# Row maximum of a 64 MiB tensor: the loads cut as 14, 14, 12, 11, 9, 8, 8, ... in two blocks, in place of 15, 14, 13, 11, ... in four

## Chip, cores and metric

One core of a Trainium2 chip. The metric is the device time of one execution in microseconds (us). The span that the profile shows is some 2 us shorter. DVE is the vector engine, which does the reductions.

## The reference

```python
x = np.random.randn(32, 512, 1024).astype(np.float32)   # drawn with a fixed seed
return np.max(x, axis=-1).astype(np.float32)            # 32 x 512 results
```

16384 rows of 1024 floats: 128 partitions with 128 rows each. Below, "a row" is one row in each of the 128 partitions, 512 KiB in all.

## The kernel before

```python
BLOCKS = [
    [15, 14, 13],
    [11, 9, 8, 7],
    [6, 6, 5, 4, 4, 4, 3, 2],
    [2, 2, 2, 2, 2, 1, 1, 1, 1, 1, 1, 1],
]
RING = 46
...
    ring = once.tile([P, RING, D], F32)
    res = once.tile([P, I], F32)
    at = first = 0
    for loads in BLOCKS:
        S = sum(loads)
        xb = xf[first * P:(first + S) * P, :].rearrange("(p i) d -> p i d", p=P)
        b = 0
        for g in loads:
            if at + g > RING:
                at = 0
            xc = ring[:, at:at + g, :]
            nc.sync.dma_start(out=xc, in_=xb[:, b:b + g, :])
            nc.vector.reduce_max(out=res[:, first + b:first + b + g], in_=xc, axis=X)
            at += g
            b += g
        dst = bass.AP(tensor=of.tensor, offset=of.offset + first * P, ap=[[S, P], [1, S]])
        nc.scalar.dma_start(out=dst, in_=res[:, first:first + S])
        first += S
```

A block of S rows gives each partition S consecutive rows, so neighbouring partitions read S x 4 KiB apart: that is the pitch. Each block ends with one output. Within a block each number is one load and one reduction. The sizes fall because a row takes longer to load than to reduce (1.204 against 1.067 us, worked out in the prediction): each reduction should last about as long as the next, smaller load.

Of the kernel before, what the change touches and what calls it, by code (L numbers as in the profile page):

```python
# [1 line left out]

# [4 lines left out]


F32 = mybir.dt.float32



BLOCKS = [
    [15, 14, 13],
    [11, 9, 8, 7],
    [6, 6, 5, 4, 4, 4, 3, 2],
    [2, 2, 2, 2, 2, 1, 1, 1, 1, 1, 1, 1],
]
RING = 46


@with_exitstack
def kernel(
    ctx: ExitStack,
    tc: tile.TileContext,
    x: bass.AP,
    out: bass.AP,
):
    nc = tc.nc
    P = 128  # L30
    X = mybir.AxisListType.X

    xf = x.flatten_outer_dims()
    N, D = xf.shape
    I = N // P
    of = out.flatten_outer_dims()

    once = ctx.enter_context(tc.tile_pool(name="once", bufs=1))
# [19 lines that stand above are left out]
    assert first == I  # L58


# [1 line left out]
_INS = ['x']  # L62
_OUTS = [((32, 512), 'float32')]


# [23 lines left out]
```

## Time and profile before

| | before |
|---|---|
| time, first three runs | 165.55 to 165.71 us, median 165.6 |
| span of the profiled run | 163.6 us |
| DVE busy, of the span | 138.4 us, 85% |
| load queue, share of 16 engines | 96.3% |
| loads, reductions, outputs | 27, 27, 4 |
| first reduction starts; last one ends | 21.39; 161.25 us |

Neither resource has slack: the stream of loads is full from 1.7 to 159.1 us, and the DVE works without a pause from 54.06 to the end.

### The profile page before, as it was taken

What the parts mean: (1) busy time and instruction counts of PE and PEld (TensorE: products, weight loads), DVE (VectorE), ACT (ScalarE), POOL (GpSimd) and SP (SyncE); (2) the same over time, 40 slices, a digit from 0 to 9 for tenths busy, and PEclk for the clock granted to TensorE, in tenths of its full rate; (3) what the DMA queues carried; (4) which work ended last, traced back from release to release, by engine and by line L of the source; (5) the groups of instructions that cost most, each with busy time, mean ns of one, the idle gap of its engine ahead of it and who ended that gap; (6) DMA issues with size and microseconds to landing.
All of it is one profiled execution on the core that took longest, in us unless ns stands there. A gap on an engine that the chain in (4) does not pass through costs nothing.

```text
span 163.6 us, 114 instructions
## 1 busy us (share of the span) xinstructions
DVE 138.4 (85%) x27; POOL 0.2 (0%) x4
## 2 busy tenths in 40 slices
DVE  0000079998999899999999999999999999999994
POOL 0000000000000000000000000000000000000000
DMA  7999699999999989999989999999999999999980
GB/s 240 481 481 436 285 449 449 449 449 417 417 417 417 529 353 529 388 425 401 459 385 465 449 401 427 439 400 459 419 421 421 445 405 421 421 421 415 409 339 2
DMA packets 4464, 67.18 MB, mean 411 GB/s; under 512 B 1008, under 2 KB 1008, under 8 KB 1904
## 3 DMA queue, kind: packets, MB, share of 16 engines
q1 hardware_dynamic: 3888, 67.11, 96.3%
q10 hardware_dynamic: 576, 0.07, 0.3%
HBM read 67.11 MB, written 0.07 MB: 411 GB/s over the span
## 4 chain that ended last, share of the span: by engine, by line
DVE 74%; DMA 23%; DVEq 1%; another core or an unknown queue 0%; SPq 0%; issue 0%
DVE res L52 74%; DMA ring<-in_x_dram 23%; DVEq L84 1%; SPq L51 0%
## 5 line engine op out<-in xcount | busy, mean ns | idle before, releaser
L52 DVE TENSOR_REDUCE res<-ring 128x1 f32<-128x1024 f32 (+12 forms) x27 | 138.4, 5205 | 22.8 <-DMA ring<-in_x_dram 22.8
L73 POOL MEMSET const-bfloat16-1.0<- 128x1 bf16 x1 | 0.1, 102 | 0.0
L73 POOL MEMSET const-uint8-127<- 128x1 uint8 x1 | 0.1, 102 | 0.0
L73 POOL MEMSET const-float32-0.0<- 128x1 f32 x1 | 0.1, 99 | 0.2 <-issue 0.2
L73 POOL MEMSET const-float32-1.0<- 128x1 f32 x1 | 0.1, 99 | 0.0
## 6 DMA issues: line engine op xcount, KB each, us to landing
ring<-in_x_dram SPq DMA_DIRECT2D x1, 7680.0 KB, 20.6
ring<-in_x_dram SPq DMA_DIRECT2D x1, 7168.0 KB, 37.2
ring<-in_x_dram SPq DMA_DIRECT2D x1, 6656.0 KB, 52.4
ring<-in_x_dram SPq DMA_DIRECT2D x2, 3072.0 KB, 33.3
ring<-in_x_dram SPq DMA_DIRECT2D x3, 2048.0 KB, 33.8
ring<-in_x_dram SPq DMA_DIRECT2D x6, 1024.0 KB, 23.9
ring<-in_x_dram SPq DMA_DIRECT2D x1, 5632.0 KB, 29.8
ring<-in_x_dram SPq DMA_DIRECT2D x1, 4608.0 KB, 24.9
```

Of the source, the lines that this page charges most:

```text
L52: nc.vector.reduce_max(out=res[:, first + b:first + b + g], in_=xc, axis=X)
L73: nc = _bacc.Bacc("TRN2", target_bir_lowering=False, num_devices=1)
L84: with _tile.TileContext(nc) as tc:
```

## The change

Its intent is to keep reductions and loads in step with one load fewer and two outputs fewer.

```diff
 BLOCKS = [
-    [15, 14, 13],
-    [11, 9, 8, 7],
-    [6, 6, 5, 4, 4, 4, 3, 2],
-    [2, 2, 2, 2, 2, 1, 1, 1, 1, 1, 1, 1],
+    [14, 14, 12, 11, 9, 8, 8, 7, 6, 5, 4, 4, 4, 3, 3],
+    [2, 2, 2, 2, 2, 1, 1, 1, 1, 1, 1],
 ]
```

Four things move at once: the load sizes, their number (27 to 26), the outputs (4 to 2), and the pitches (168, 140, 136 and 68 KiB become 448 and 64 KiB).

## The prediction

> **What bounds the kernel now.** I read the page first: busy time by engine and the transfer queues, for which resource is full.
>
> ```profile
> span 163.6 us, 114 instructions
> DVE 138.4 (85%) x27; POOL 0.2 (0%) x4
> ...
> q1 hardware_dynamic: 3888, 67.11, 96.3%
> q10 hardware_dynamic: 576, 0.07, 0.3%
> ```
>
> The load queue (q1) is full for 96.3% of the span, the vector engine (DVE) for 85%. So this is a stream of 64 MiB with a reduction running behind it. To see whether the stream ever pauses I asked for the stretch from its first packet (1.7 us) to its last (159.1 us). The columns are stretch, length, DVE busy, POOL busy, clock, transfer share, GB/s.
>
> ```profile
> 1.70:159.10 157.40, 136.28 (x26) 0.00 (x0) 1.00 1.00 427
> ```
>
> It does not pause: share 1.00. The dip near the fifth slice of the page's timeline is only how packets are binned by their start. Next, the chain of waits that ended last, in order of time.
>
> ```profile
> 0.73 0.37 SPq L51
> 1.10 0.05 issue
> 1.15 37.16 DMA ring<-in_x_dram
> 38.31 0.02 issue
> 38.33 15.09 DVE res L52
> 53.42 0.61 another core or an unknown queue
> 54.03 0.02 issue
> 54.06 106.07 DVE res L52 x24
> 160.12 1.13 DVEq L84
> ```
>
> From 54.06 us on the DVE never waits: 25 reductions end at 161.25. So the end is set by the third load's landing (54.03) plus all work after it, although the stream is also full until 159.1. The two bounds nearly touch: by the trace's semaphore record the last one-row load landed at 159.57, and its reduction started at 160.03, when the one before let it, only 0.46 us later. Last, cost per shape (shape, busy and mean ns, idle before it).
>
> ```profile
> L52 DVE TENSOR_REDUCE res<-ring 128x15 f32<-128x15360 f32 x1 | 16.2, 16153 | 21.4 <-DMA ring<-in_x_dram 21.4
> L52 DVE TENSOR_REDUCE res<-ring 128x14 f32<-128x14336 f32 x1 | 15.1, 15087 | 0.8 <-DMA ring<-in_x_dram 0.8
> L52 DVE TENSOR_REDUCE res<-ring 128x13 f32<-128x13312 f32 x1 | 14.0, 14020 | 0.6 <-DMA ring<-in_x_dram 0.6
> ```
>
> A row more costs 16153 - 15087 = 1066 ns. The 0.8 and 0.6 us are the DVE waiting for loads 2 and 3; nothing later has idle time.
>
> **What the Trainium skill says.** "VectorE: DVE Perf Modes", section "The perf-mode tier table (the rule you actually need)": tensor_reduce has only the 1x program. With the 0.96 GHz that the page gives, 1024 elements are 1067 ns; the trace's 1066 agrees, so cutting the loads otherwise cannot make a row cheaper. "DMA: Bandwidth & Descriptors", section "Where 436 GB/s comes from", gives a ceiling of 435 GB/s; the trace moves 427 over the whole stream, so only 2% is left there, part of which is overhead per descriptor. The same page, section "Latency and other measured facts", reports row pitches of large powers of two that slow copies between HBM tensors: 207 GB/s per direction at 512 KiB against 214 for a padded one, 164 at 2 MiB. That bears on the new blocks, whose pitch is 112 x 4 = 448 KiB and 16 x 4 = 64 KiB per partition, against 168, 140, 136 and 68 before. The trace before has nothing on it: its four blocks run at one rate.
>
> **A model from the trace.** Let n be rows landed and k loads landed. Three landings, 38.31 (29 rows, 2 loads), 54.03 (42, 3) and 159.57 (128, 27), give two slopes. From 54.03 - 38.31 = 15.72 = 13a + b and 159.57 - 54.03 = 105.54 = 86a + 24b follow a = 1.204 us per row and b = 0.08 per load; the constant is then 3.22. So landing = 3.22 + 1.204n + 0.084k. For load 1 this gives 21.36, as in the trace, and the landings of loads 4, 7 and 20 come out within 0.1 us (67.36, 96.50, 150.56 against 67.36, 96.54, 150.63).
>
> The DVE's cadence: 107.19 us from 54.06 to 161.25 for 99 rows in 25 reductions. 99 x 1.0665 = 105.58, which leaves 1.61 / 25 = 0.064 us per reduction. (The mean of a one-row reduction, 1216 ns, is longer than its cadence of 1.13: neighbours overlap by about 0.09.)
>
> Each load puts a floor under the end of the last reduction: its landing + 0.03 + 1.0665 x (rows not before it) + 0.064 x (reductions not before it). The largest floor is the end. For the kernel before the floors of loads 1 to 4 are 159.63, 160.51, **161.25**, 160.64. Later ones that stand high are load 13 (160.63), load 20 (160.70) and the last (160.73). So only one load is badly placed, the third with 13 rows: it costs 0.52 us above the floor of the very last load.
>
> **The change, part by part.**
>
> *The first three loads*, 14, 14, 12 in place of 15, 14, 13. Load 1 lands at 20.16, 1.2 earlier, and the DVE starts earlier; but it then waits longer for load 2 (28 rows, 37.09; the first reduction ends about 35.3), so that gain is eaten by a wait of near 1.9 us. Load 3 (40 rows) lands at 51.62, when the DVE is still at load 2 until 52.1. Floors: 158.36, 160.31, 159.84. The binding 161.25 is gone.
>
> *The middle*, 11, 9, 8, 8, 7, 6, 5, 4, 4, 4, 3, 3 in place of 11, 9, 8, 7, 6, 6, 5, 4, 4, 4, 3. Floors: load 4 160.30, load 7 (the second 8) 160.60, load 8 160.51, load 13 (the last 4, 106 rows) 160.57. All are close and none exceeds 160.6.
>
> *The end*, five of 2 and six of 1 in place of six and seven. The last 2 (122 rows, 20 loads) lands at 151.76, floor 151.79 + 8 x 1.0665 + 7 x 0.064 = **160.77**; the last row's floor is 160.65.
>
> *One load and one reduction fewer*: 0.08 us of stream and 0.064 of DVE, already in the floors.
>
> *Two outputs in place of four.* In the transfer records an output's data packets took 15 ns (168 B), 14, 14 and about 11 each, 8 per transfer engine, plus 36 ns in all of semaphore writes: some 0.47 us of the stream for all four, of which 0.38 came before the last load landed. One output of 448 B per partition, perhaps 25 ns a packet (an estimate by extending 168 B to 448), is 0.2 us beside the loads. So up to 0.15 us of stream is saved. The last output (64 B per partition) should land 1.4 us after issue, as the 68 B one did. The tail is unchanged.
>
> Sum: the largest floor goes from 161.25 to 160.77, which is 0.48 us less, and a little more through the outputs: 0.5 to 0.6. In place of one load that was too early, seven stand within 0.3 us of the maximum (loads 7, 8, 13, 19, 20, 25 and 26), so the DVE will show several tiny waits, not none. 165.6 - 0.5 = 165.1 us.
>
> **Rivals.**
>
> *The ring or a semaphore starves the stream.* The instruction order shows the waits of each load. With ring places counted off, load 4 reuses load 1's place (free at 35.4, while the stream is busy with load 3 until 51), load 5 needs reduction 2 (52.2; stream busy with load 4 to 64.5), load 7 reduction 3 (65; loads 5 and 6 cover to 85). Later loads wait for the landing of a load about eight earlier. The new one to fear: load 25 waits for the first output, which goes out near 143 when the fifteenth reduction ends. The third output of the kernel before, issued at 142.43, took 6.5 us to land among two-row loads; so 149.5, and load 25 is not due in the stream before 156.5. Margin 7 us. If I am wrong there, each us of pause is a us of time.
>
> *The new pitch slows the reads.* If 3% (207 against 214, an estimate from that page) struck the 112-row block, 135 us of stream become 139: 169 to 170 us, slower by over 2%. Against it: 448 KiB is 7 x 64 KiB and no power of two, and the blocks before, with pitches from 68 to 168 KiB, do not differ in rate. A few tenths of a per cent are possible too.
>
> *The stream is the bound at the end and nothing is gained.* The last row's floor before was 160.73, so no order of loads can gain more than about 0.5 us; if the outputs or the single rows cost more than fitted, only 0 to 0.2 us come out: 165.4 to 165.6.
>
> *A larger gain from the earlier start.* The page shows 21.4 us of idle DVE before the first reduction; a reader may hope for 1.2 us from a start that early. The wait for load 2 takes it back: the sum of rows to come is bounded by the stream.
>
> **Range and chances.** The three runs before lie within 0.16 us and the model hits the landings within 0.1, so the mechanism alone gives 164.8 to 165.5. I widen to 164.5 below, for cheaper outputs, and 166.0 above, for a slight loss from the pitch. 2% is 3.3 us: no saving of that size exists in a stream already at 1.00, so faster gets 0.01. Slower needs the pitch effect or a starved stream: 0.05. Within 2%: 0.94.
>
> **What would show it right or wrong.** Right: first reduction at 20.2, an idle of about 1.9 before the second, no large wait before the third; DVE work ending at 160.6 to 160.8; stream share 1.00 again; span near 163.1. Wrong: a GB/s below 425 in the first 140 us (pitch), a stretch with share well under 1.00 near 150 to 157 (load 25 held by the output), or a DVE wait of over 0.5 us after the second reduction.

## The result, and the profile after

The changed kernel took 165.1 us (median of 6 runs, 165.0 to 165.22); before in the same rounds 165.66 (6 runs, 165.5 to 165.79). The ratio is 0.9967, with a 95% interval of 0.9954 to 0.998: a gain that is clear of noise, of a third of a per cent. Ratios here are the mean time of one kernel's runs over that of the other's of the same rounds, so not quite the ratio of the quoted medians.

The page after, busy time and queues:

```profile
span 163.3 us, 109 instructions
DVE 138.5 (85%) x26; POOL 0.2 (0%) x4
...
q1 hardware_dynamic: 3744, 67.11, 96.4%
q10 hardware_dynamic: 288, 0.07, 0.2%
```

The totals have hardly moved: the same bytes at the same share, the same DVE work. The same stretch of the stream as before (stretch, length, DVE busy, POOL busy, clock, transfer share, GB/s):

```profile
1.70:159.10 157.40, 136.72 (x25) 0.00 (x0) 1.00 1.00 427
```

Still full, at the same 427 GB/s. What moved is the chain that ended last (start, length, what):

```profile
1.15 35.88 DMA ring<-in_x_dram
37.03 0.02 issue
37.05 58.02 DVE res L50 x5
95.07 0.02 issue
95.08 36.77 DMA ring<-in_x_dram
131.85 0.02 issue
131.87 19.94 DMA ring<-in_x_dram
151.81 0.02 issue
151.84 7.92 DVE res L50 x6
159.75 1.13 DVEq L82
```

Before, this chain left the stream for good at 54 us. Now it goes back to the stream until 151.81, where the load that brings the rows landed to 122 lands. Two bounds alternate, which is what a well-cut pipeline looks like. The timeline of the DVE (start, length, what, count, and in brackets the idle time before it):

```profile
20.11 15.09 DVE L50 TENSOR_REDUCE res<-ring 128x14 f32<-128x14336 f32 x1 [20.11 <-DMA ring<-in_x_dram]
37.05 58.00 DVE L50 TENSOR_REDUCE res<-ring 128x14 f32<-128x14336 f32 x5 [1.85 <-DMA ring<-in_x_dram]
95.28 56.37 DVE L50 TENSOR_REDUCE res<-ring 128x8 f32<-128x8192 f32 x13 [0.22 <-DMA ring<-in_x_dram]
...
151.84 9.04 DVE L50 TENSOR_REDUCE res<-ring 128x2 f32<-128x2048 f32 x7 [0.19 <-DMA ring<-in_x_dram]
```

The DVE starts 1.28 us earlier than before and then waits 1.85 us for the second load; it does not wait for the third. It ends at 160.88 (151.84 + 9.04) against 161.25 in the profiled runs.

The two traces show less than the whole gain: the profiled run of the kernel before took 165.37 us, less than all six timed ones, and that of the change 165.1. So they differ by 0.27 us where the timed medians differ by 0.56. No trace shows the rest; a start of the stream that varies at the old pitch (below) may hold a part of it.

### The profile page after: what moved, and what is told of

It is laid out like the page before. It is cut to its first block, busy times and chain, and to the rows that moved or that the text cites. A ratio compares the mean times of both kernels' runs of the same rounds, so it can differ in the third digit from the quotient of the medians.

```text
span 163.3 us, 109 instructions
## 1 busy us (share of the span) xinstructions
DVE 138.5 (85%) x26; POOL 0.2 (0%) x4
## 4 chain that ended last, share of the span: by engine, by line
DMA 57%; DVE 40%; DVEq 1%; SPq 0%; issue 0%
DMA ring<-in_x_dram 57%; DVE res L50 40%; DVEq L82 1%; SPq L49 0%
## 5 line engine op out<-in xcount | busy, mean ns | idle before, releaser
L50 DVE TENSOR_REDUCE res<-ring 128x1 f32<-128x1024 f32 (+11 forms) x26 | 138.5, 5396 | 22.4 <-DMA ring<-in_x_dram 22.4
```

## The experiments

The theory is that each load sets a floor (its landing plus all reductions left), the highest floor is the end, and the change lowers it from load 3's 161.25 to load 20's 160.77. The rivals are that the outputs saved, the load saved, or the new pitch give the gain. Diffs are against the kernel before where not said otherwise. "Landing" is the semaphore time of a load in the trace; the first reduction starts 0.02 us after load 1 lands.

**1. One load two rows too large (dose).**

```diff
-    [15, 14, 13],
+    [14, 13, 15],
```

> The kernel before with its first block cut 14, 13, 15 in place of 15, 14, 13: same rows, same number of loads, outputs and bytes, only the third load is two rows larger. Theory: load 3 lands at the same 54.03 us but two rows more are then left, so the end moves by 2 x 1.0665 = 2.13 us: highest floor 163.38, time 167.7 to 167.8, ratio 1.013, and the last row lands at 159.6 as before, that is some 2.6 us before its reduction starts. Rival (the stream alone sets the end): time stays at 165.6, ratio 1.000.

Measured: 167.78 us (167.38 to 167.99) against 165.6 for the kernel before, ratio 1.0124 (1.0106 to 1.0142). The DVE's timeline:

```profile
20.67 15.09 DVE L52 TENSOR_REDUCE res<-ring 128x14 f32<-128x14336 f32 x1 [20.67 <-DMA ring<-in_x_dram]
36.41 14.02 DVE L52 TENSOR_REDUCE res<-ring 128x13 f32<-128x13312 f32 x1 [0.66 <-DMA ring<-in_x_dram]
54.55 109.32 DVE L52 TENSOR_REDUCE res<-ring 128x15 f32<-128x15360 f32 x25 [4.12 <-DMA ring<-in_x_dram]
```

The time rose by 2.18 us where two rows make 2.13. The wait before load 3's reduction grew from 0.64 to 4.12 us and was never won back: the last load lands at 160.05 and its reduction starts 2.61 us later. In this profiled run, the slowest of the four, the stream was late from load 1 on, so load 3 landed at 54.52 and not at 54.03, and the last row at 160.05 and not at 159.6 (more on this below). With the same bytes, loads, outputs and pitches, and the same 42 rows landed by load 3, two rows more of work behind that landing move the end by two rows. A bound by the stream alone is refuted.

**2. Only the first block recut.**

```diff
-    [15, 14, 13],
+    [14, 14, 12, 2],
```

> The kernel before with its first block cut 14, 14, 12, 2; all later loads and the four outputs as before (28 loads). Theory: the floor of load 3 drops to 159.97, and what is left is that of the last row and of the last 2-row load, 160.82 and 160.78, because of one load more: time 165.1 to 165.3, ratio 0.997 to 0.998. So nearly the whole gain of the change comes back from the first block alone. Rival (middle, end, or outputs of the change carry the gain): 165.6 or, with one load more, 165.7, ratio 1.000.

Measured: 165.06 us (164.88 to 165.3) against 165.6, ratio 0.9963 (0.9948 to 0.9977). The whole gain is there, with four outputs, the old pitches and even one load more than before (28). So neither outputs, pitch nor number of loads is needed for it. Its DVE timeline shows the wait at load 3 gone, and in its place a small one of 0.20 us at the next large load, the one of 11 rows:

```profile
37.30 30.14 DVE L52 TENSOR_REDUCE res<-ring 128x14 f32<-128x14336 f32 x3 [1.86 <-DMA ring<-in_x_dram]
...
67.64 93.46 DVE L52 TENSOR_REDUCE res<-ring 128x11 f32<-128x11264 f32 x24 [0.20 <-DMA ring<-in_x_dram]
```

**3. The changed loads in four blocks.** Same 26 loads as the change, cut after rows 40, 76 and 112:

```diff
-    [15, 14, 13],
-    [11, 9, 8, 7],
-    [6, 6, 5, 4, 4, 4, 3, 2],
-    [2, 2, 2, 2, 2, 1, 1, 1, 1, 1, 1, 1],
+    [14, 14, 12],
+    [11, 9, 8, 8],
+    [7, 6, 5, 4, 4, 4, 3, 3],
+    [2, 2, 2, 2, 2, 1, 1, 1, 1, 1, 1],
```

> The 26 loads of the changed kernel, but in four blocks of 40, 36, 36 and 16 rows, so four outputs and pitches of 160, 144, 144 and 64 KiB. Theory (the floor of each load, set by the stream and the reductions left, decides the end): the highest floor is still that of load 20, 160.77 us, so the DVE ends at 160.8 to 160.95 and the time is 165.1 to 165.25, ratio to before 0.997. Rival (the two outputs fewer carry the gain): the time goes back to 165.5 to 165.6, ratio 0.999 to 1.000. Rival (the pitch of 448 KiB costs something that the gain hides): the time falls below 165.0.

Measured: 165.38 us (165.21 to 165.74), ratio 0.9985 (0.9971 to 0.9999). A miss: half of the gain went, as neither the theory nor a rival had it. The first lines of its DVE timeline show where:

```profile
20.48 15.09 DVE L52 TENSOR_REDUCE res<-ring 128x14 f32<-128x14336 f32 x1 [20.48 <-DMA ring<-in_x_dram]
37.41 58.00 DVE L52 TENSOR_REDUCE res<-ring 128x14 f32<-128x14336 f32 x5 [1.83 <-DMA ring<-in_x_dram]
```

Everything is as in the change, shifted by some 0.36 us from the very first landing (20.48 against 20.11, 37.41 against 37.05). Outputs cannot do that: the first one leaves at 65 us.

**4. The old loads in two blocks.**

```diff
-    [15, 14, 13],
-    [11, 9, 8, 7],
-    [6, 6, 5, 4, 4, 4, 3, 2],
+    [15, 14, 13, 11, 9, 8, 7, 6, 6, 5, 4, 4, 4, 3, 2],
     [2, 2, 2, 2, 2, 1, 1, 1, 1, 1, 1, 1],
```

> The 27 loads of the kernel before, in two blocks of 111 and 17 rows, so two outputs and long pitches (444 and 68 KiB). Theory: load 3 still lands at 54.03 us and its floor of 161.25 us holds the end; time 165.5 to 165.7, ratio 0.999 to 1.001. Rival (outputs carry the gain): 165.1 to 165.3, ratio 0.997 to 0.998. Rival (pitch slows the reads): landings later than the model by over 0.3 us at load 14, time above 165.8.

Measured: 165.94 us (165.86 to 166.05), ratio 1.0017 (1.0002 to 1.0031). The rival of the outputs falls, as two outputs fewer gained nothing. But the time was 0.3 us above the theory. Load 1 landed at 21.75 against 21.37 in the kernel before and the third load at 54.38 against 54.03: again a shift made before the first landing. The signs named for slow reads came true (a time above 165.8, and load 14 landing 0.3 us late), yet the reads are not slower: from the first landing to the last the stream took 138.17 us, against 138.20 in the kernel before.

**5. Chance or layout? The last two again, beside the change.** The same kernels, together with the change itself, in rounds of their own.

> The changed kernel itself, as a reference on the same chip and in the same rounds as the three below. Expected ratio to before 0.997 (0.9954 to 0.998 in its first measurement), time near 165.1 us.

> The four-block version of the changed loads once more. It came out 0.25 us above what its floors said, and its first load landed 0.3 us after the model (20.46 against 20.16) and every later load with it. If that late start is chance from run to run (which of the 16 transfer engines gets its first packet done last), this run lands load 1 at 20.1 to 20.5 with no relation to the layout and the ratio is 0.997 again, as for the changed kernel. If two outputs more or the pitch of 160 KiB cost it, the ratio is 0.9985 again, and the changed kernel beside it has 0.997.

> The old loads in two blocks (111 and 17 rows) once more. It was 0.3 us slower than the kernel before, in all 5 of its runs, with the first load landing 0.38 us late and all later ones by the same amount. If chance: ratio 0.999 to 1.001. If the layout (pitch of 444 KiB) delays the start of the stream: load 1 lands at 21.7 to 21.8 again and the ratio is 1.0015 to 1.002 again.

Measured: the change 165.11 us (165.06 to 165.14), ratio 0.9969 (0.9957 to 0.9982). Four blocks 165.29 (165.26 to 165.56), ratio 0.9984 (0.9972 to 0.9997). The old loads in two blocks 165.98 (165.86 to 166.14), ratio 1.0022 (1.0009 to 1.0036). Load 1 landed at 20.11, 20.38 and 21.82: as in the first runs, within 0.1 us. First reduction of the old loads in two blocks, this run:

```profile
21.84 16.15 DVE L50 TENSOR_REDUCE res<-ring 128x15 f32<-128x15360 f32 x1 [21.84 <-DMA ring<-in_x_dram]
```

So for these layouts it is not chance from run to run: each shift came again on another chip. The start of the stream goes with how the rows are laid out over the partitions.

**6. The changed layout with four outputs.** Against the change: blocks as they are, results written after rows 40, 76, 112 and 128.

```diff
-    at = first = 0
+    at = first = done = 0
...
-        dst = bass.AP(tensor=of.tensor, offset=of.offset + first * P, ap=[[S, P], [1, S]])
-        nc.scalar.dma_start(out=dst, in_=res[:, first:first + S])
+            if first + b in (40, 76, 112, 128):
+                n = first + b - done
+                dst = bass.AP(tensor=of.tensor, offset=of.offset + first * P + done - first, ap=[[S, P], [1, n]])
+                nc.scalar.dma_start(out=dst, in_=res[:, done:first + b])
+                done = first + b
```

> The changed kernel with its two blocks (pitch 448 and 64 KiB) left as they are, but the results written in four pieces, after rows 40, 76, 112 and 128. If the four outputs were what cost 0.25 us in the four-block runs, ratio 0.9985 and time 165.3 to 165.4. If it was the later start of the stream with the other pitch (160 KiB), load 1 lands at 20.1 and the ratio stays 0.997, time 165.1 to 165.2.

Measured: 165.01 us (164.91 to 165.2) against 165.5 for the kernel before in these rounds, ratio 0.9972 (0.996 to 0.9984).

```profile
20.04 15.09 DVE L50 TENSOR_REDUCE res<-ring 128x14 f32<-128x14336 f32 x1 [20.04 <-DMA ring<-in_x_dram]
36.98 57.99 DVE L50 TENSOR_REDUCE res<-ring 128x14 f32<-128x14336 f32 x5 [1.85 <-DMA ring<-in_x_dram]
```

Four outputs cost nothing that can be seen. From the first landing to the last the stream took 139.31 us with four (20.02 to 159.33) and 139.38 with two (20.09 to 159.46).

**7. The changed layout with the old early loads.** Against the change:

```diff
-    [14, 14, 12, 11, 9, 8, 8, 7, 6, 5, 4, 4, 4, 3, 3],
+    [15, 14, 13, 11, 9, 8, 7, 6, 6, 5, 4, 4, 4, 3, 3],
```

> The early loads of the kernel before (15, 14, 13, 11, 9, 8, 7, 6, 6, 5, ...) and the late ones of the change, in the change's two blocks of 112 and 16 rows, so its pitch of 448 KiB, its two outputs and its 26 loads. Theory: the floor of load 3 (161.18 us) holds the end again, so the sizes of the first loads are the gain and pitch, outputs and number of loads are not: time 165.4 to 165.6, ratio 0.999 to 1.000. The two-block run with a pitch of 444 KiB was at 1.002; if two blocks as such made that, this run is at 1.001 to 1.002 and lands load 1 at 21.7 or later; if it was that one pitch, load 1 lands at 21.2 to 21.4. Rival (pitch or outputs are the gain): ratio 0.997.

Measured: 165.37 us (165.3 to 165.6) against 165.5, ratio 0.9997 (0.9985 to 1.0009). The gain is gone, with the change's pitch, outputs and number of loads all in place. Its DVE timeline is that of the kernel before, wait at load 3 and all:

```profile
21.32 16.15 DVE L50 TENSOR_REDUCE res<-ring 128x15 f32<-128x15360 f32 x1 [21.32 <-DMA ring<-in_x_dram]
38.26 15.09 DVE L50 TENSOR_REDUCE res<-ring 128x14 f32<-128x14336 f32 x1 [0.79 <-DMA ring<-in_x_dram]
53.99 107.13 DVE L50 TENSOR_REDUCE res<-ring 128x13 f32<-128x13312 f32 x24 [0.64 <-DMA ring<-in_x_dram]
```

Together with experiment 2 this closes the main question: recutting the early loads is enough for the gain (2) and the gain does not come without it (7). At one layout it is worth 0.9997 - 0.9967 = 0.003 of 165.5 us, so 0.5 us (0.4 with the 0.9972 of experiment 6, taken in the same rounds, where no run of one reaches those of the other: 165.3 to 165.6 against 164.91 to 165.2); the floors say 161.18 - 160.77 = 0.41. The kernel before was some 0.1 us faster in these rounds than in the earlier ones, and the times of experiments 6 and 7 lie just under those expected; the ratios are as expected. Experiment 7 also refutes that two blocks as such start the stream late.

**8. Pitch of 512 KiB, and of 408.** The changed loads in one block of 128 rows; and cut after row 102.

> The 26 loads of the changed kernel in one block of 128 rows per partition, so a pitch of 512 KiB, a large power of two, and one output of 512 B per partition after the last reduction. Theory (floors, and no effect of the pitch at this read-only rate): landings as in the changed kernel, DVE ends near 160.9, the last output takes 1.4 to 1.7 us; time 165.0 to 165.4. Rival (the pitch slows reads by some 3%, as the page on DMA reports for copies between HBM tensors): landings late by up to 4 us, time 168 to 170.

> The 26 loads of the change with the cut between the blocks after row 102 instead of 112: pitches 408 and 104 KiB, still two outputs. Only the layout of the reads moves. If the start of the stream depends on the pitch, load 1 lands anywhere from 20.1 to 20.6 but alike in all runs, and the time follows it one to one: 165.0 to 165.6. If pitch has no effect and the two earlier layouts were chance: load 1 at 20.1 and 165.1.

Measured, one block: 165.55 us (165.48 to 165.75), ratio 0.9998 (0.9985 to 1.001), a miss: 165.0 to 165.4 was expected. Its first reduction and its stream:

```profile
20.57 15.09 DVE L49 TENSOR_REDUCE res<-ring 128x14 f32<-128x14336 f32 x1 [20.57 <-DMA ring<-in_x_dram]
...
1.70:159.10 157.40, 136.38 (x25) 0.00 (x0) 1.00 1.00 426
```

The rate is untouched (426 GB/s against 427), so the feared 3% is refuted; but the start is 0.46 us late, of which 0.29 is left when the DVE ends (161.17 against 160.88), and the single output lands 1.57 us after issue instead of 1.42. Together that is the 0.44 us by which it is slower than the change beside it (165.11), nearly the whole gain. At 408 KiB load 1 landed at 20.09 and the DVE ended at 160.89, as in the change; the time was 165.22 us (165.14 to 165.37), ratio 0.9986 (0.9974 to 0.9998). That is 0.1 us above its own profiled run (165.14) and 0.2 above experiment 6 in the same rounds; the intervals of the ratios overlap, and this difference stays open. As load 1 landed where the change has it, this run could not tell an effect of the pitch from none.

**What makes the late start.** The trace's transfer records name no engine, but from 3 to 158 us at least 15 packets are under way at any time in every profile, so the 16 transfer engines seem to run from their first packet on without a gap. Load 1 lands when the slowest is through. In all nine profiled runs whose first load has 14 rows it lands 15.13 to 15.16 us after the last of the 16 first packets ends, whatever the layout: the late start is the lateness of that packet. It ended at 4.95 us in the change (the eighth of the 16 at 4.76), at 5.32 in the four-block run (4.62), at 5.53 in the old loads in two blocks (4.84, with 15 rows), at 5.40 in the one block (4.86). Some of these packets begin late, others take longer than the rest. The lateness then stays: in the four-block run the last of a load's 16 semaphore increments comes 0.32 us after the one before it at load 1, and still 0.30 us at load 26. Landings of load 1 by pitch of the first block, as excess over the model of the prediction (20.16 for 14 rows, 21.36 for 15):

| pitch, KiB | excess in the profiled runs, us |
|---|---|
| 448 | -0.07, -0.05, -0.14, -0.07 |
| 408 | -0.07 |
| 160 | +0.30, +0.22 |
| 444 | +0.39, +0.46 |
| 512 | +0.39 |
| 168 | 0.00, +0.17, +0.48 |

All but 168 repeat where they were tried twice; 408 and 512 have one profile each. The three values at 168, the pitch of the kernel before, come from three different kernels (before, experiments 2 and 1), so whether the start varies there from run to run is not shown. The wider spread of the kernel before would fit it: 165.41 to 166.07, 165.5 to 165.72 and 165.24 to 165.85 in three sets of rounds, against 165.0 to 165.22 and 165.06 to 165.14 for the change. Why one pitch starts evenly and another not was not found: no simple rule in the pitch is visible in six values.

No version beats the change clearly. Experiment 2 (165.06) and experiment 6 (165.01) tie with it. By the floors there is little left: the last row's own floor is 160.65, 0.12 under the highest, and a search over all sequences of whole rows in that sum finds none below 160.71.

## Why the prediction was right, step by step

- *The model.* Solved exactly, the two equations as printed give 1.202 us per row and 0.089 per load, not 1.204 and 0.084. That moves no floor by more than 0.05 us, and the landings of the change came out within 0.1 us of the model.
- *The bound.* That load 3 held the end was right: the end followed its size in experiment 1 and the gain vanished with its return in experiment 7.
- *The first loads.* First reduction at 20.11 (predicted 20.2), 1.85 us of idle before the second (near 1.9), none before the third: right, and so the rival of a gain from the earlier start was rightly refused.
- *Middle and end.* The highest floor was named as load 20's: the trace has the DVE's last wait there. Of the "several tiny waits" two show, 0.22 us at load 7 and 0.19 at load 20. Load 20 landed at 151.81 for a predicted 151.76, and the DVE ended at 160.88, 0.1 above the sum and just outside the 160.6 to 160.8 given as a sign. Load 19, which lands (149.33) about when the first output does (149.51), shows part of why: 2.63 us after load 18 where two rows otherwise take 2.49, so the output of 448 B per partition seems to have cost 0.14 us there (estimated at 0.2). The tail, called unchanged, grew too: from the end of the DVE to the end of the span 2.44 us, before 2.35. So the span is 163.3 and not near 163.1; why the tail grew is open.
- *Outputs.* "Up to 0.15 us of stream is saved" did not come: experiment 6 shows no gain from two outputs fewer. The packets of 448 B took the 25 ns that were estimated; what failed is the step from their time to time of the stream. Two large outputs cost the stream about what four small ones do.
- *The semaphore rival.* Load 25 was issued at 149.53, with the first output's landing at 149.51, as worked out, and landed at 158.21 for a predicted 158.20. No starvation; share 1.00.
- *The pitch rival.* It was right to keep it and wrong in form. It is not the rate that depends on the layout but the start: up to half a microsecond once, the same size as the gain. The change happens to have a layout that starts evenly. At 512 KiB the same loads took 165.55 (experiment 8): the number would have missed by 0.4, though inside the range.

The number (165.1) and the mechanism hold; part of its exactness is luck with the layout.

## What to carry to other kernels

In a stream with a consumer a little faster than it, write down for every load the floor (landing plus work left) and cut the sizes until the floors are level: here first loads of 15, 14, 13 in place of 14, 14, 12 cost 0.4 us, two rows more in the third cost 2.2. A consumer that starts earlier gains nothing if the next load then makes it wait. And look at the first landing of each variant before comparing ends: a layout can shift the whole run by some tenths, which hides or feigns a gain of that size.

## What the Trainium skill lacked or had wrong

- "DMA: Bandwidth & Descriptors", section "Latency and other measured facts", gives 207 GB/s for copies between HBM tensors at a row pitch of 512 KiB, 3% less than the 214 of a padded pitch. It has no such row for loads into SBUF. For those, from one core, the runs show no loss of rate: 426 GB/s at 512 KiB, 427 at 448 and at 168.
- No page that was consulted has the effect of the layout on the start of a stream: load 1 of 14 rows lands at 20.02 to 20.11 us with pitches of 448 and 408 KiB, at 20.38 to 20.55 with 160 and 512. The slowest of the 16 first packets ends 0.5 to 0.7 us after the eighth of them with the latter pitches, 0.2 to 0.3 us with the former.
